# Six of eight tiles ahead in linear attention's out-projection, and root chains given other engines and delays

## The chip, the core and the metric

One core of one Trainium2 chip runs the kernel. Its engines are TensorE (PE, matrix products, with its weight loads shown apart as PEld), VectorE (DVE), ScalarE (ACT), GpSimd (POOL) and SyncE (SP, which here issues the loads of weights). The metric is the device time of one execution in microseconds (us), the median of several runs. Lower is better.

## The reference

A decoder trunk of two layers works on 512 tokens behind 16 meta tokens, 528 rows of width 1024, in float32. Layer 0 mixes tokens by gated linear attention in chunks (GLA, four heads), layer 1 by local attention with a window of 128, learned sinks and shared keys and values (SWA). Around each mixer stand two feed-forward blocks (FFN), and each sublayer is normalised at its input and at its output:

```
for layer in range(2):
    h = h + 0.5 * rmsnorm(swiglu(rmsnorm(h, g[0]), w_in0, w_out0), g[1])
    hn = rmsnorm(h, g[2])
    mix = gla_mixer(hn, ...) if layer == 0 else swa_mixer(hn, ...)
    h = h + rmsnorm(mix, g[3])
    h = h + 0.5 * rmsnorm(swiglu(rmsnorm(h, g[4]), w_in1, w_out1), g[5])
    if layer == 0:
        k_sh, v_sh = shared_kv(h, ...)

# the end of gla_mixer, per head of 256 columns
o = rmsnorm(o, g_head) * silu(r)
return o.reshape(B, L, 1024) @ w_out
```

`rmsnorm` divides by the root of the mean square over the columns. In `gla_mixer` that mean is taken for each head by itself.

## The kernel before

**Layout.** Columns lie on partitions, tokens along the free axis. A matrix of width 1024 is thus eight tiles of 128 partitions. In layer 0 the tokens are cut into two groups, `L0`, of 272 and 256; in layer 1 the norms use `L1`, two groups of 256, and the products mostly `L1W`, one of 512.

**Products.** Each float32 product is made of three matmuls of rounded halves (`mm3`): high weight by high input, low weight by high input, high weight by low input. The high half of an input or a weight is a copy by ACT (L413, L432, L228), the low half a subtraction by DVE (L414, L433, L229). The third matmul of a product needs the low half of the input.

**Order.** PE runs in the order in which the program emits its matmuls; nothing reorders them. The program is a planner: `Flow` keeps a clock that each emitted matmul moves forward by its own length, and side jobs, written as generators, yield a delay and are resumed when the clock has passed it. A job that yields 2.0 therefore emits its next matmul about 2 us of matrix work later, whether or not its input is there by then. If it isn't, PE stands still. The order on ACT, DVE, POOL and SP is made by a scheduler. PSUM gives eight banks in rotation, the weights have 32 slots and a ring of eight raw buffers filled by SP.

**A norm.** The squares of the tiles are made on ACT. With one part (`parts` of 1) all squares of a group end in one sum: ACT writes the first square into it (L405), the others go to a scratch tile (L408) and POOL adds them (L409). With two parts the last square stays alone in a second sum, so POOL has no last addition and PE sums two tiles. `rstd` then emits: the column sums by PE (`st_`), a chain of small steps for the reciprocal root (`av_`, `yv_`, `zv_`, `wv_`, L366 to L386), a diagonal matrix (`dg_`, L388), and, after a planned delay, a matmul that spreads the factors over the partitions (`r_`). The chain runs on POOL (then its first step is on ACT, L368; planned delay `CHAIN`, 5) or on DVE (`DCHAIN`, 3). `Operand.factors` uses it for the factor R of a block's input, copied from PSUM by ACT (L449), on POOL. `Residual.run` uses it on DVE for a block's output, and then for each of eight tiles multiplies and adds on DVE (L471, L472), makes the next input's halves (L432, L433) and its squares.

**The end of GLA.** The four heads' cores run one after the other while PE also projects `x` by the gate's weights, eight units of two groups (`x<-x_l0m`). For the last head (h = 3) the order is: the head's output in two banks (`po_`, copied to `Y` by ACT at L977) and a small one for the meta tokens (`pn`, copied by DVE at L980), squares, `st_go`, roots on POOL for both groups, `r_go` for both groups, and DVE's scaling of `Y` (L989). `gated` makes `rg` from the gate (L1005 to L1007), and when the head is scaled, multiplies by the gain and by `Y` (L1012) and splits the result into the halves of `og`, one for each of the eight tiles. The tiles 0 to 3 belong to heads 0 and 1 and wait for their cores; the tiles 4 to 7 all wait for the last head's. `flow.wait(*jobs)` ends this stage, and only then `out_proj` opens: each of its units takes eight tiles of `og` into one bank, 24 matmuls (`y<-og`).

**out_steps** can be told of jobs that are still open (`jobs`): it then opens the first three banks (m, group) with all tiles but the last, waits for these jobs, and goes on. GLA doesn't use this before the change.

**SWA.** `x_first` projects queries by unit; the first four need R (`r_l1m`) before DVE can make `q` from them (L1036 to L1039, with POOL). Scores (`sc`) go to PE between the rows of the next four units (`x<-x_l1m`), whose matmuls fill PE's time there. Then `out_proj` runs twice, and at its end the norm of its output `post_l1f`: group 0's tiles are finished first, then group 1's, so group 0's `Residual.run` goes on during group 1's products, and the next block's input `x_l1f` is made tile by tile.

Of the kernel before, what the change touches and what calls it, by code (L numbers as in the profile page):

```python
# [17 lines left out]
D = 1024  # L18
KD = 8
# [7 lines left out]
HEADS = 4  # L27
RSQRT_MAGIC = float(0x5F3759DF)
L0 = [(0, 272), (272, 256)]
L1 = [(16, 256), (272, 256)]  # L30
# [14 lines left out]
STAGGER = 5.0  # L45
SOFT = 5.0
ADDED = 1.4
BEHIND = 2.2
NORM = 3.0
LAG = 3  # L50
# [75 lines left out]
def trunk_kernel(ctx: ExitStack, tc, a, out):  # L126
    nc = tc.nc
    pe, act, dve, pool, sp = nc.tensor, nc.scalar, nc.vector, nc.gpsimd, nc.sync
    flow = Flow()
# [8 lines left out]
    Y = cp.tile([P, KD, TOK], F32, name="Y")  # L138
# [20 lines left out]
    def gain(layer, i, k):  # L159
        c = V_GAIN + layer * 48 + i * 8 + k  # L160
        return vec[:, c : c + 1]
# [43 lines left out]
    used, asked, freed, ahead, cap, dma_end = [0], [0], [0], [16], [len(units)], [0.0]  # L205
# [143 lines left out]
    def mm3(o, w, j, x, g, start, stop):  # L349
        mm3s([(o, w)], j, x, g, start, stop)  # L350
# [50 lines left out]
    def square_into(sums, src, i, count, name, parts=2):  # L401
        n = src.shape[-1]
        if i == 0 or i == count - 1 and parts == 2:
            sums.append(sm.tile([P, 272], F32, tag="acc", name=f"acc_{name}", bufs=6))
            act.activation(sums[-1][:, :n], src, AF.Square)  # L405
            return
        t = sm.tile([P, 272], F32, tag="sq", name=f"sq_{name}", bufs=2)
        act.activation(t[:, :n], src, AF.Square)  # L408
        pool.tensor_tensor(sums[0][:, :n], sums[0][:, :n], t[:, :n], op=ALU.add)  # L409
# [6 lines left out]
    class Operand:  # L416


        def __init__(self, name, gv, groups, rt=None, parts=(1, 2)):
            self.parts = parts  # L420
            self.name, self.gv, self.groups, self.tiles = name, gv, groups, [None] * KD
            self.ready = set()
            self.rt = rt
            self.rjob = [None] * len(groups)
            self.accs = [[] for _ in groups]
# [17 lines left out]
        def factors(self, gi, eng=pool):  # L443
            if self.rt is None:
                self.rt = sm.tile([P, TOK], F32, tag="R", name=f"R_{self.name}", bufs=2)
            o, n = self.groups[gi]
            yield FACT + (ADDED if self.parts[gi] == 1 else 0)
            r = yield from rstd(self.accs[gi], n, D, False, f"{self.name}_{o}", eng, gi * BEHIND if eng is dve else 0.0)
            act.activation(self.rt[:, o : o + n], r[:, :n], AF.Copy)  # L449

        def need(self, gi, k):
# [1 line left out]


    class Residual:
        def __init__(self, name, layer, i, half, nxt=None):
            self.name, self.half, self.nxt = name, half, nxt
            self.gain = lambda m: gain(layer, i, m)

        def run(self, gi, g, sums):  # L460
            o, n = g
            nxt = self.nxt
            yield 1.8 + (0 if gi else ADDED)
            r = yield from rstd(sums, n, D, self.half, f"post_{self.name}{gi}", dve)
            if nxt is None:
                yield from self.store(gi, g, r)
                return
            for k in range(KD):
                h, y = H[:, k, o : o + n], Y[:, k, o : o + n]
                t = r[:, 256 : 256 + n] if n <= 256 else ps(f"t_{self.name}{gi}{k}")[:, :n]  # L470
                dve.tensor_tensor(t, y, r[:, :n], op=ALU.mult)  # L471
                dve.tensor_tensor(h, t, h, op=ALU.add)  # L472
                nxt.build(gi, k)
                nxt.sumsq(gi, k)
                yield 1.0
            nxt.rjob[gi] = flow.spawn(nxt.factors(gi), gi * BEHIND)
# [81 lines left out]
    def out_proj(*args, **named):  # L558
        for _ in out_steps(*args, **named):
            pass  # L560

    def out_steps(hid, groups, split_groups, first, finish=None, tailm=0, packed=False, jobs=()):
        nh = len(hid)
        ws = []

        def tile_of(m, j):
            i, c = divmod(m * nh + j, 8) if packed else (m, j)
            while len(ws) <= i:
                ws.append(next_w())
            return ws[i], c  # L570

        begun = {}

        def begin(m, g):
            o, n = g
            p = begun[m, o] = ps(f"y{used[0]}_{m}_{o}")
            for j, t in enumerate(hid[:-1]):
                w, c = tile_of(m, j)
                mm3(p[:, :n], w, c, t, g, j == 0, False)

        def unit(m, g):
            o, n = g
            if (m, o) not in begun:
                begin(m, g)
            p = begun[m, o]
            w, c = tile_of(m, nh - 1)
            mm3(p[:, :n], w, c, hid[-1], g, nh == 1, True)
            y = Y[:, m, o : o + n]
            if first:
                act.activation(y, p[:, :n], AF.Copy)  # L590
            else:
                dve.tensor_tensor(y, p[:, :n], y, op=ALU.add)  # L592

        accs = [[], []] if finish else []

        def sq(m, gi):
            o, n = split_groups[gi]
            y = Y[:, m, o : o + n]
            square_into(accs[gi], y, m, KD, f"post{used[0]}_{m}_{gi}", gi + 1)
            act.activation(y, y, AF.Identity, scale=finish.gain(m))  # L600

        def through(m):
            return (m + 1) * nh // 8 if packed else m + 1

        freed = 0
        if jobs:
            order = [(m, g) for m in range(KD - tailm) for g in groups]
            order += [(m, split_groups[0]) for m in range(KD - tailm, KD)]
            begin(*order[0])
            yield  # L610
            for m, g in order[1 : 2 if order[1][1][1] == SEQ else 3]:
                begin(m, g)
            flow.wait(*jobs)
        for m in range(KD - tailm):
            for g in groups:
                unit(m, g)
            done_w(through(m) - freed)
            freed = through(m)
            for gi in range(len(accs)):
                sq(m, gi)  # L620
        if not finish:
            return
        for gi, g in enumerate(split_groups):
            for m in range(KD - tailm, KD):
                unit(m, g)
                sq(m, gi)
                if gi:
                    done_w(through(m) - freed)
                    freed = through(m)
            flow.spawn(finish.run(gi, g, accs[gi]))  # L630
# [187 lines left out]
    def gla(x, finish):  # L818
        set_ahead(10)
        with tc.tile_pool(name="gp", bufs=1) as gp:  # L820
# [59 lines left out]
            blk = lambda t: t[:, META:].rearrange("p (b c) -> p b c", c=P)  # L880

            def core(h, before):
                for j in before:
                    yield j
                tau = 1.0 / 16.0
# [7 lines left out]
                for i in range(2):  # L893
                    p = ps(f"pv{h}_{i}")
# [32 lines left out]
                p = ps(f"pk{h}")  # L927
# [13 lines left out]
                p = ps(f"pa{h}")  # L941
# [40 lines left out]
                for gi, (o, n) in enumerate(L0):  # L982
                    accs.append([])
                    for i in range(2):
                        square_into(accs[gi], Y[:, 2 * h + i, o : o + n], i, 2, f"go{h}_{gi}", 1)
                yield 2.0 + ADDED
                def scale(gi, o, n):
                    r = yield from rstd(accs[gi], n, 256, True, f"go{h}_{gi}", more=BEHIND)
                    dve.tensor_tensor(  # L989
                        yy[:, :, o : o + n], yy[:, :, o : o + n],  # L990
                        r[:, :n].unsqueeze(1).to_broadcast([P, 2, n]), op=ALU.mult,
                    )
# [32 lines left out]
            jobs = []  # L1025
            set_ahead(8)
            x_units(x, KD, L0, lambda i, g, p: jobs.append(flow.spawn(gated(i, g, p))))
            flow.wait(*jobs)
            set_ahead(16)
            cap[0] = used[0] + 12  # L1030
            out_proj(og, L0, L0, True, finish, 5)

    def rope(dst, p, c, s, name):
        n = dst.shape[-1]
# [244 lines left out]
    dve.memset(eps, 1e-6)  # L1279
    dve.tensor_scalar(hident, ident, 0.5, None, op0=ALU.mult)  # L1280

    def into(name, layer, i, half, gv, groups, parts=(1, 2)):
        nxt = Operand(name, gv, groups, parts=parts)
        return nxt, Residual(name, layer, i, half, nxt)


    nxt, fin = into("l0m", 0, 1, True, lambda k: gain(0, 2, k), L0, (1, 1))
# [9 lines left out]
    with tc.tile_pool(name="kp", bufs=1) as kp:  # L1297
        x = Operand("l1f0", lambda k: gain(1, 0, k), L1)

        def again(gi):  # L1300
            for k in range(KD):
                x.build(gi, k)
                yield 1.0

        kv, placed = shared_kv(nxt, kp, [again(0), again(1)])
        x.rt, x.rjob = nxt.rt, nxt.rjob
        nxt, fin = into("l1m", 1, 1, True, lambda k: gain(1, 2, k), L1, (1, 1))
        ffn(x, L1W, fin)
        x = nxt
        nxt, fin = into("l1f1", 1, 3, False, lambda k: gain(1, 4, k), L1)  # L1310
        flow.wait(placed)
        swa(x, kv, fin)
    ffn(nxt, L1W, Residual("out", 1, 5, True))
# [85 lines left out]
```

## Time and profile before

| what | value |
|---|---|
| time, median of 3 runs | 1918.19 us (1917.45 to 1920.05) |
| the profiled execution's own time | 1915.33 us |
| its span, first to last instruction | 1913.5 us |
| PE busy | 1872.4 us, 98% |
| DVE, ACT, POOL busy | 1420.2, 1002.8, 236.6 us |
| mean granted TensorE clock | 0.996 |

The profiled execution is 2.86 us below the median, and 1.83 us of its time lie around the span. In a timeline row stand the start, the length, the engine, the line, the operation, the written tile and the read ones, the shape, how many such instructions follow each other, and in brackets how long the engine had been idle and what ended it. In a row of waits stand the total, the number of times and the longest. In a row by windows stand the window, its length, the busy time of each engine with its count, the granted clock, the share of DMA and its rate.

### The profile page before, as it was taken

To read this page: it belongs to the slowest core of one execution; us is meant where nothing else is said; L and a number is where in the kernel's file an instruction comes from. 1 tells how busy PE (TensorE), PEld (TensorE's weight loads), DVE (VectorE), ACT (ScalarE), POOL (GpSimd) and SP (SyncE) were. 2 spreads that over 40 slices of the span, in tenths; PEclk is the share of its full clock that TensorE was granted. 3 is DMA by queue.
4 is the path that set the end of the run, shared out by engine and by line. 5 is a ranking of instruction groups with operands and counts; after the bars stand their busy time and mean duration, and the time that the engine had idled before them with its cause. 6 is when DMAs were issued, how large, how long until landed. Compare 5 with 4: busy or idle time off the path is not lost.

```text
span 1913.5 us, 37141 instructions
## 1 busy us (share of the span) xinstructions
PE 1872.4 (98%) x14374; PEld 1786.8 (93%) x14374; DVE 1420.2 (74%) x2868; ACT 1002.8 (52%) x2268; POOL 236.6 (12%) x439
## 2 busy tenths in 40 slices
PE   8999999999999999999999999999998999999997
PEld 8999999999998999999999898989976888989897
DVE  7885858775564798585887886868789578868584
ACT  5663636663245566363674553536646555536363
POOL 2000000321122400000034000000361140000002
PEclk9999999999999999999999999999999999999999
DMA  4332333322123123233351223233320212233331
GB/s 165 99 101 94 101 99 102 120 78 78 45 59 108 45 79 101 93 102 97 102 170 45 67 91 113 91 108 110 118 78 23 78 45 72 95 105 106 105 116 45
DMA packets 102017, 174.60 MB, mean 91 GB/s; under 512 B 11345, under 2 KB 24145, under 8 KB 101841
## 3 DMA queue, kind: packets, MB, share of 16 engines
q1 hardware_dynamic: 101008, 171.59, 28.4%
q8 instruction: 112, 1.84, 0.4%
q10 hardware_dynamic: 832, 0.65, 0.1%
q14 instruction: 65, 0.52, 0.1%
HBM read 170.10 MB, written 2.10 MB: 90 GB/s over the span
## 4 chain that ended last, share of the span: by engine, by line
PE 79%; DVE 13%; ACT 3%; issue 2%; POOL 1%; DMA 0%; DVEq 0%; ACTq 0%; POOLq 0%
PE y L164 29%; PE a L164 18%; PE x L164 14%; PE c L164 8%; PE d L164 4%; DVE raw L253 2%; DVE w L229 2%; ACT w_s L247 1%; DVE w_s L248 1%; DVE w L248 1%; PE e L164 1%; PE o L164 1%; PE po L164 1%; PE ps L164 0%; DVE H L472 0%
## 5 line engine op out<-in xcount | busy, mean ns | idle before, releaser
L248 DVE TENSOR_TENSOR w_s<-raw,w_s 128x512 fp32r<-128x512 f32 x288 | 193.9, 690 | 124.4 <-ACT w_s L247 122.4
L164 PE MATMUL y<-hidl0f,w 128*128 128x256 f32 (+1 forms) x2112 | 261.7, 285 | 0.8 <-DVE hidl0f L414 0.6
L164 PEld LDWEIGHTS y<-hidl0f,w 128*128 128x128 f32 x2112 | 258.9, 188 | 1.6 <-DVE hidl0f L414 1.0
L229 DVE TENSOR_TENSOR w<-raw,w 128x512 fp32r<-128x512 f32 x378 | 242.1, 670 | 17.7 <-ACT w L228 15.8
L247 ACT ACTIVATE w_s<-raw 128x512 fp32r<-128x512 f32 x288 | 175.3, 628 | 146.0 <-DVE raw L253 142.4
L164 PE MATMUL y<-hidl1f,w 128*128 128x512 f32 (+1 forms) x1344 | 249.9, 346 | 0.3
L164 PEld LDWEIGHTS y<-hidl1f,w 128*128 128x128 f32 x1344 | 212.7, 188 | 33.6 <-DVE hidl1f L811 0.7
L409 POOL TENSOR_TENSOR acc_post<-acc_post,sq_post 128x256 f32<-128x256 f32 (+1 forms) x78 | 63.3, 811 | 1360.2 <-ACT sq_post L408 1359.7
L228 ACT ACTIVATE w<-raw 128x512 fp32r<-128x512 f32 x378 | 208.0, 586 | 36.9 <-PE y L164 26.0
L253 DVE TENSOR_TENSOR raw<-raw,raw 128x512 f32<-128x512 f32 x288 | 197.9, 687 | 5.5
L248 DVE TENSOR_TENSOR w<-raw,w 128x512 fp32r<-128x512 f32 x216 | 148.3, 687 | 40.0 <-ACT w L247 39.1
L247 ACT ACTIVATE w<-raw 128x512 fp32r<-128x512 f32 x216 | 134.0, 621 | 48.0 <-PE y L164 47.7
L164 PE MATMUL x<-x_l0m,w 128*128 128x272 f32 (+1 forms) x1200 | 158.1, 288 | 0.0
L164 PEld LDWEIGHTS x<-x_l0m,w 128*128 128x128 f32 x1200 | 149.2, 188 | 1.0
L592 DVE TENSOR_TENSOR Y<-y,Y 128x256 f32<-128x256 f32 (+2 forms) x176 | 82.3, 473 | 76.6 <-PE y L164 75.9
L164 PE MATMUL a<-zl0f_t,w_s 128*128 128x264 f32 x864 | 117.5, 285 | 0.0
L164 PE MATMUL a<-zl1f_t,w_s 128*128 128x256 f32 x864 | 114.7, 282 | 0.9 <-ACT c L786 0.7
L164 PEld LDWEIGHTS a<-zl0f_t,w_s 128*128 128x128 f32 x864 | 110.3, 188 | 0.3
L164 PEld LDWEIGHTS a<-zl1f_t,w_s 128*128 128x128 f32 x864 | 107.5, 188 | 2.3 <-ACT c L786 1.7
L164 PE MATMUL x<-x_l0f,w 128*128 128x256 f32 (+1 forms) x768 | 99.5, 290 | 7.6 <-ACT w L228 6.4
L164 PEld LDWEIGHTS x<-x_l0f,w 128*128 128x128 f32 x768 | 96.4, 191 | 8.8 <-ACT w L228 6.4
L164 PE MATMUL x<-x_l1f,w 128*128 128x256 f32 (+1 forms) x576 | 94.0, 321 | 1.9 <-ACT x_l1f L432 1.8
(485 smaller groups left out, 3290.7 us busy)
## 6 DMA issues: line engine op xcount, KB each, us to landing
raw<-in_w_in SPq DMA_DIRECT2D x352, 256.0 KB, 2.9
raw<-in_w_out SPq DMA_DIRECT2D x96, 256.0 KB, 3.4
raw<-in_gla_in SPq DMA_DIRECT2D x50, 256.0 KB, 3.4
raw<-in_w_last SPq DMA_DIRECT2D x48, 256.0 KB, 3.0
raw<-in_w_out SPq DMA_DIRECT2D x64, 128.0 KB, 3.0
raw<-in_gla_out SPq DMA_DIRECT2D x16, 256.0 KB, 2.7
raw<-in_w_q SPq DMA_DIRECT2D x16, 256.0 KB, 4.0
raw<-in_swa_out SPq DMA_DIRECT2D x16, 256.0 KB, 2.8
```

What stands on the lines that cost most here:

```text
L164: inst = pe.matmul(o, lhs, rhs, start=start, stop=stop, skip_group_check=onto)
L228: act.activation(w[:, 0, :m], raw[:, :m], AF.Copy)
L229: dve.tensor_tensor(w[:, 1, :m], raw[:, :m], w[:, 0, :m].bitcast(F32), op=ALU.subtract)
L247: act.activation(w[:, 0, :512], src, AF.Copy)
L248: dve.tensor_tensor(w[:, 1, :512], src, w[:, 0, :512].bitcast(F32), op=ALU.subtract)
L253: dve.tensor_tensor(dst, dst, src, op=ALU.add)
L409: pool.tensor_tensor(sums[0][:, :n], sums[0][:, :n], t[:, :n], op=ALU.add)
L592: dve.tensor_tensor(y, p[:, :n], y, op=ALU.add)
```

## The change

It has four parts.

- `LONGER`, 0.8, is added to the planned delay of a root chain on POOL in `Operand.factors`. The `r_` matmul of every block input that has its chain there is emitted later by that much matrix work.
- `Residual` gets its own `parts`, and `into` a parameter for them (`post`). For the norm of the local attention's output it is (2, 2) in place of (1, 2): group 0's squares end in two sums, and its `st_` is planned 1.4 us sooner. The other norms keep (1, 2).
- For the last head of GLA the squares end in two sums for both groups, `st_go` is planned 1.4 us sooner, and the roots run on DVE, both groups' steps taking turns, with the delay of DVE's chains and 2.2 more for the second group.
- GLA waits only for the first twelve jobs (tiles 0 to 5) before `out_proj`, which gets the open jobs and `late=2`: the first three banks are opened with six tiles each, the last two tiles of each follow.

```
+LONGER = 0.8
 class Operand / factors:
-            r = yield from rstd(..., eng, gi * BEHIND if eng is dve else 0.0)
+            r = yield from rstd(..., eng, gi * BEHIND if eng is dve else LONGER)
 class Residual:
-        def __init__(self, name, layer, i, half, nxt=None):
+        def __init__(self, name, layer, i, half, nxt=None, parts=(1, 2)):
+            self.parts = parts
-            yield 1.8 + (0 if gi else ADDED)
+            yield 1.8 + (ADDED if self.parts[gi] == 1 else 0)
 out_steps:
-    def out_steps(hid, groups, split_groups, first, finish=None, tailm=0, packed=False, jobs=()):
+    def out_steps(hid, groups, split_groups, first, finish=None, tailm=0, packed=False, jobs=(), late=1):
-            for j, t in enumerate(hid[:-1]):
+            for j, t in enumerate(hid[:-late]):
-            w, c = tile_of(m, nh - 1)
-            mm3(p[:, :n], w, c, hid[-1], g, nh == 1, True)
+            for j in range(nh - late, nh):
+                w, c = tile_of(m, j)
+                mm3(p[:, :n], w, c, hid[j], g, j == 0, j == nh - 1)
-            square_into(accs[gi], y, m, KD, f"post{used[0]}_{m}_{gi}", gi + 1)
+            square_into(accs[gi], y, m, KD, f"post{used[0]}_{m}_{gi}", finish.parts[gi])
 gla / core:
+                last = h == HEADS - 1
-                        square_into(accs[gi], Y[:, 2 * h + i, o : o + n], i, 2, f"go{h}_{gi}", 1)
-                yield 2.0 + ADDED
+                        square_into(accs[gi], Y[:, 2 * h + i, o : o + n], i, 2, f"go{h}_{gi}", 1 + last)
+                yield 2.0 + (0 if last else ADDED)
-                    r = yield from rstd(accs[gi], n, 256, True, f"go{h}_{gi}", more=BEHIND)
+                    eng, more = (dve, gi * BEHIND) if last else (pool, BEHIND)
+                    r = yield from rstd(accs[gi], n, 256, True, f"go{h}_{gi}", eng, more)
 gla, its end:
-            flow.wait(*jobs)
+            flow.wait(*jobs[:12])
-            out_proj(og, L0, L0, True, finish, 5)
+            out_proj(og, L0, L0, True, finish, 5, jobs=jobs, late=2)
 the calls:
-    def into(name, layer, i, half, gv, groups, parts=(1, 2)):
+    def into(name, layer, i, half, gv, groups, parts=(1, 2), post=(1, 2)):
-        return nxt, Residual(name, layer, i, half, nxt)
+        return nxt, Residual(name, layer, i, half, nxt, post)
-        nxt, fin = into("l1f1", 1, 3, False, lambda k: gain(1, 4, k), L1)
+        nxt, fin = into("l1f1", 1, 3, False, lambda k: gain(1, 4, k), L1, post=(2, 2))
```

More of the change, by code (lines that the diff above doesn't have):

```diff
@@ L447, in factors @@
             yield FACT + (ADDED if self.parts[gi] == 1 else 0)
-            r = yield from rstd(self.accs[gi], n, D, False, f"{self.name}_{o}", eng, gi * BEHIND if eng is dve else 0.0)
+            r = yield from rstd(self.accs[gi], n, D, False, f"{self.name}_{o}", eng, gi * BEHIND if eng is dve else LONGER)
             act.activation(self.rt[:, o : o + n], r[:, :n], AF.Copy)
```

## The prediction

> **What bounds the kernel now.** I read the page's busy shares, then PE's waits, then the timeline at the three places that the change touches, and the granted clock there by windows. First the page and the waits of PE:
>
> ```profile
> PE 1872.4 (98%) x14374; PEld 1786.8 (93%) x14374; DVE 1420.2 (74%) x2868; ACT 1002.8 (52%) x2268; POOL 236.6 (12%) x439
> ...
> PE 79%; DVE 13%; ACT 3%; issue 2%; POOL 1%; DMA 0%; DVEq 0%; ACTq 0%; POOLq 0%
> ```
>
> ```profile
> PE r_go L164 <- POOL dg_go L388: 4.2, 1, 4.2
> ...
> PE x L164 <- ACT x_l1f L432: 1.8, 2, 1.3
> PE sc L164 <- DVE q L1037: 1.6, 1, 1.6
> ...
> PE r_post_l1f L164 <- DVE dg_post_l1f L388: 0.8, 1, 0.8
> ...
> PE r_kv L164 <- POOL dg_kv L388: 0.5, 1, 0.5
> PE r_l0f L164 <- POOL dg_l0f L388: 0.3, 1, 0.3
> ```
>
> PE is busy 98% of the span, and 79% of the chain that ended last is PE. The matrix work stays but for a few small column sums. So what can be won is idle PE, a few microseconds out of 1913.5, and it is worth its full length where PE is what ends the stage. The longest wait that the change can touch is the last GLA head's `r_go`, 4.2 us. The clock, by windows (window, length, then busy us of PE, PEld, DVE, ACT, POOL, granted clock, DMA share, rate):
>
> ```profile
> 577.80:581.20 3.40, 0.73 (x2) 0.30 (x2) 0.75 (x3) 1.03 (x4) 3.22 (x12) 1.00 0.49 154
> 581.20:584.60 3.40, 3.36 (x13) 3.18 (x14) 2.78 (x7) 0.00 (x0) 0.00 (x0) 0.50 0.00 0
> ...
> 1420.90:1424.30 3.40, 1.76 (x11) 1.05 (x10) 3.40 (x9) 1.46 (x5) 3.24 (x5) 1.00 0.51 154
> 1424.30:1427.70 3.40, 3.40 (x11) 2.33 (x11) 3.40 (x6) 1.16 (x4) 3.32 (x3) 0.50 0.22 77
> ```
>
> Behind the idle stretch at `r_go` PE ran 3.4 us at half clock, and again in the attention behind a stretch in which it was busy 1.76 of 3.40 us. Each such window costs half of its 3.4 us, 1.7 us of work.
>
> [...]
>
> **A. The end of GLA.** The timeline of PE, then of the other engines:
>
> ```profile
> 568.04 0.39 PE L164 MATMUL pn<-am,vm 16*128 16x16 f32 x2
> 568.36 5.01 PE L164 MATMUL x<-x_l0m,w 128*128 128x272 f32 x39
> 573.21 1.04 PE L164 MATMUL st_go<-ones,acc_go 128*68 128x1 f32 x12
> 574.11 2.06 PE L164 MATMUL x<-x_l0m,w 128*128 128x256 f32 x15
> 580.40 2.06 PE L164 MATMUL r_go<-dg_go,ones 68*128 68x272 f32 x4 [4.23 <-POOL dg_go L388]
> 581.90 4.11 PE L164 MATMUL y<-og,w 128*128 128x272 f32 x20
> ...
> 586.19 10.02 PE L164 MATMUL y<-og,w 128*128 128x272 f32 x78 [0.17 <-DVE og L414]
> ```
>
> ```profile
> 569.04 0.78 DVE L1005 TENSOR_TENSOR rg<-x,R_l0m 128x272 f32<-128x272 f32 x2 [0.38 <-PE x L164]
> ...
> 574.18 0.19 POOL L369 TENSOR_SCALAR yv_go<-av_go 68x4 int32<-68x4 int32 x1 [3.13 <-ACT av_go L368]
> ...
> 579.71 0.64 POOL L388 TENSOR_TENSOR dg_go<-hident,yv_go 68x272 f32<-68x272 f32 x1
> ...
> 581.16 0.72 DVE L989 TENSOR_TENSOR Y<-Y,r_go 128x544 f32<-128x544 f32 x1 [2.65 <-PE r_go L164]
> ...
> 583.11 1.12 DVE L414 TENSOR_TENSOR og<-rg,og 128x272 fp32r<-128x272 f32 x3
> ```
>
> What is lost there now: the `x` row of 39 takes 573.21 - 568.36 = 4.85 us, 0.124 us a matmul. From the end of `x` (574.11 + 2.06 = 576.17) to the end of the `y` row (586.19 + 10.02 = 596.21) are 20.04 us. In them lie four records of `r_go`, about 0.5 us at that rate, and 98 matmuls of `y` (20 and 78), 12.2 us. So 7.3 us are lost: 4.2 in the wait for POOL, 1.7 by the half clock, the rest inside `r_go` and on `og`.
>
> POOL's chain is why: 574.18 to 580.35 is 6.2 us for two groups, with 2.1 us of `x` as its cover. After the change the chain is on DVE. Of DVE's chain for one group the trace shows the first and last of ten steps and the diagonal, and one pair of independent small steps:
>
> ```profile
> 381.32 0.16 DVE L366 TENSOR_SCALAR av_post_l0m<-st_post_l0m 128x2 f32<-128x2 f32 x1 [1.68 <-PE st_post_l0m L164]
> ...
> 383.29 0.43 DVE L388 TENSOR_TENSOR dg_post_l0m<-hident,yv_post_l0m 128x256 f32<-128x256 f32 x1
> ```
>
> ```profile
> 431.27 0.16 DVE L913 TENSOR_TENSOR f<-b 128x16 f32<-128x16 f32 x1
> 431.36 0.54 DVE L914 TENSOR_TENSOR f<-b 128x384 f32<-128x384 f32 x1
> ```
>
> A group takes 383.29 - 381.32 = 1.97 us and 0.43. Two groups whose steps take turns take between 1.97 us (each second step fits into the gap of the first, as the 0.09 us between L913 and L914 suggests) and 3.94 us (each step waits for the one in front). With 0.2 us of hand-over that is 2.6 to 4.6 us from `st_go` to `dg_go`. In the built order 27 matmuls of `x` stand between `pn` and `st_go` and 21 between `st_go` and `r_go`: 21 x 0.124 = 2.6 us of cover. The wait at `r_go` is then 0 to 2.0 us; I take 0.3, since the nearer row is the pair of independent steps.
>
> Then PE meets `og`. In DVE's built order the low half of tile 4 stands behind `rg` of unit 7 (two of L1005, 0.78), both scalings of `Y` (0.72 and about 0.7) and two gate steps between them (0.4 each), and takes 0.42 itself (a third of the 1.12 row, rounded up): 3.5 us after the last `x`. PE gets there after two `r_go` (0.5) and 14 matmuls (1.7): 1.3 us of waiting, and 0.4 on tile 5, two subtractions later. The tiles 6 and 7 are needed only after 54 matmuls (6.7 us), and by the same steps are there about 2 us sooner. This is what the six-tile opening is worth: it covers the last head's own tiles, not the halves of tiles 4 and 5, which are queued behind its scaling. `st_go` doubles from 12 records to 24, at (574.11 - 573.21) / 12 = 0.075 us: +0.9. POOL's 26 lost instructions and the ACT steps gone are worth nothing by themselves, as nobody else waits for them there. The raw buffers of the pair of weights that ACT now splits ahead of the last `po_` copy were issued some 25 us earlier, and SP's order stays but for one small load; I cost both at 0, and up to 0.5 if ACT is held up.
>
> Sum of A: -7.3 + 0.9 + 0.3 + 1.3 + 0.4 = -4.4 us. Best end, without waits beyond 0.5: -5.9. Worst, with a wait of 2.0, 1.8 on `og` and 0.5 on ACT: -2.1.
>
> [...]
>
> **B. `LONGER`.** `r_l0f` and `r_kv` stand 0.8 us later and no longer wait for POOL: -0.3 and -0.5 by the rows of waits above. The others had no wait at their `r_`, and R comes that much later to DVE, with eight banks behind it. -0.8, which is the best end too; the worst is 0.
>
> **C. The attention's opening.** The same delay puts `r_l1m` of the second group six matmuls later.
>
> ```profile
> 1407.10 5.78 PE L164 MATMUL x<-x_l1m,w 128*128 128x512 f32 x24
> ...
> 1410.69 0.61 POOL L388 TENSOR_TENSOR dg_l1m<-ident,yv_l1m 128x256 f32<-128x256 f32 x1
> 1410.85 0.01 DVE L1036 LOAD_MASK_SELECT sh_q<-x  x1 [3.51 <-PE x L164]
> ...
> 1419.57 2.25 DVE L229 TENSOR_TENSOR w<-raw,w 128x512 fp32r<-128x512 f32 x2
> ...
> 1424.03 2.35 PE L164 MATMUL sc<-kz,q 64*128 64x272 f32 x8 [1.64 <-DVE q L1037]
> ```
>
> Here `dg_l1m` was ready at 1411.30 and there was nothing to win: six matmuls at 5.78 / 24 = 0.24 us are 1.4 us by which R and DVE's work behind it come later. Against that, one pair of weights (2.25 us of DVE) now stands ahead of R, in the 3.51 us in which DVE was idle. So the late `q` for which PE waited 1.64 us comes 2.25 - 1.4 = 0.8 us sooner: -0.8. Best end: the wait and the half-clock window behind it both go, -3.3. Worst: the lateness stays, +1.4.
>
> **D. The norm behind the attention.**
>
> ```profile
> 1565.24 1.61 PEld L164 LDWEIGHTS x<-x_l1f,w 128*128 128x128 f32 x12 [0.69 <-ACT x_l1f L432]
> ...
> 1567.18 1.47 PEld L164 LDWEIGHTS x<-x_l1f,w 128*128 128x128 f32 x12 [0.34 <-ACT x_l1f L432]
> ```
>
> ```profile
> 1564.37 0.42 ACT L408 ACTIVATE sq_l1f<-H 128x256 f32<-128x256 f32 x1 [2.52 <-POOL acc_l1f L409]
> ...
> 1570.14 3.09 PE L164 MATMUL x<-x_l1f,w 128*128 128x256 f32 x18 [1.28 <-ACT x_l1f L432]
> ```
>
> ACT stood 2.52 us behind POOL, which was running group 0's root chain for `l1f`, and PE then waited three times for tiles of group 1, 0.69 + 0.34 + 1.28 = 2.3 us. With two sums POOL has one addition less, and group 0's `st_` and `r_post_` stand 15 matmuls earlier, 1.8 us at 0.12. Group 0's tiles and the root chain then end some 2 us sooner and ACT is free: the three waits go. Two more column sums are four records, 0.3 us at the 0.075 above; I take 0.4, as all are of the larger shape. The 0.8 us at the second `r_post_l1f` stays, its chain is not moved. -2.3 + 0.4 = -1.9; ends -2.3, and +0.5 if ACT is late again and only the records are added.
>
> **Sum.** -4.4 - 0.8 - 0.8 - 1.9 = -7.9 us against the profiled execution's own 1915.33, so 1907.4. That execution lies 2.86 us below the median of the runs; -7.9 from 1918.19 gives 1910.3, which I predict.
>
> **Rivals.** (1) DVE's two chains cost twice one, so `r_go` still waits 2.0 us, and the halves of tile 4 come as late: A is -2.8, the sum -6.3, 1911.9. For it: the pair L913/L914 had no dependence on a step just before. (2) The attention gives it back. DVE is without a gap there from R on; R is 1.4 late, the two rows of `x` that stand earlier (3 matmuls each, 1.4 us) are missing as fillers later, and one more half-clock window (1.7) is drawn: C is +4.5, the sum -2.6, 1915.6, within 0.2%. Against it: the 2.25 us moved out of the way. (3) Slower: in the attention the stalls of PE grow by the missing fillers so that windows of 3.4 us fall to half use and more, as at 1420.90. Each costs 1.7 us. With R late and the fillers gone (2.8) and five such windows (8.5), C is +11.3 and the sum +4.2: 1922.4. With three windows the gain is gone (+0.8), with five it is slower by over 0.2%. Against it: the trace shows one such window in the attention although several stalls of over a microsecond stand there.
>
> [...]
>
> **How the numbers follow.** The forecast has 0.58, (1) 0.16, (2) 0.15, (3) 0.11. 0.2% of 1918.19 is 3.8 us, about what a measurement can tell from no change; faster means below 1914.4. Forecast and (1) are faster: 0.74 with little left over; (2) is the same, 0.15; (3) slower, 0.11. The ends of A to D add up to -12.3 (1905.9) and -0.2 (1918.0), where all would have to fall the same way; the range 1906.0 to 1917.0 leaves out those corners and (3). The likeliest case alone has 1907.5 to 1913.
>
> **What would show it.** A: `r_go` with a wait under 0.5 us, none by POOL; the granted clock at 1.00 behind it; 1.7 us of waits of `y` on `og` in two or three pieces, on tiles 4 and 5. B: `r_l0f` and `r_kv` gone from PE's waits. C: DVE's weight pair in front of R; `sc` waiting under 1 us. D: no `x` waiting on `x_l1f`, and ACT no longer 2.5 us behind POOL. It goes wrong if the halves of `og` come later than 3.5 us after `x`, if the stalls of the attention grow behind the later R, or if a new half-clock window appears.

## The result and the profile after

The changed kernel takes 1910.58 us (median of 5 runs, 1909.31 to 1911.01) against 1917.52 us (median of 5 runs, 1916.36 to 1920.05): 6.9 us less, a ratio of 0.9961 with a 95% interval from 0.9946 to 0.9975. The forecast was 1910.3 us, by a sum of -7.9 us. The profiled execution took 1910.46 us, its span is 1908.6 us.

From its page, the busy shares and the chain that ended last, by engine:

```profile
PE 1873.1 (98%) x14390; PEld 1789.5 (94%) x14390; DVE 1423.5 (75%) x2890; ACT 1001.4 (52%) x2266; POOL 228.2 (12%) x412
...
PE 86%; DVE 10%; ACT 2%; issue 1%; DMA 0%; SPq 0%; DVEq 0%; ACTq 0%
```

PE runs 16 matmuls more, the column sums, and is busy 0.7 us more in a span 4.9 us shorter. Its share of the chain grew from 79% to 86%, and POOL's 1% is gone. PE's waits, only those of the places in question, first of the changed kernel, then two of the kernel before:

```profile
PE ptm L177 <- DVE mt L1176: 4.8, 1, 4.8
...
PE sc L165 <- DVE Y L1158: 2.0, 1, 2.0
PE r_post_l1f L165 <- DVE dg_post_l1f L389: 1.4, 1, 1.4
...
PE y L165 <- DVE hidl0f L415: 0.9, 3, 0.3
```

```profile
PE ptm L176 <- DVE mt L1171: 3.8, 2, 2.4
...
PE y L164 <- DVE hidl0f L414: 0.6, 2, 0.3
```

The waits of `r_go`, `r_kv` and `r_l0f` and the two of `x` on `x_l1f` are no longer in the list. New or longer are, in the attention, one of 4.8 us for `mt` in place of two, one of `sc` for DVE's `Y`, 2.0 us, in place of the 1.6 for `q`, and those of `x` for ACT's tiles of `x_l1m`, 1.2 us in place of 0.7; further the second `r_post_l1f`, 1.4 us in place of 0.8, and `y` for the FFN's hidden tiles, 0.9 in place of 0.6. The end of GLA on PE:

```profile
569.05 3.55 PE L165 MATMUL x<-x_l0m,w 128*128 128x272 f32 x27
572.44 1.98 PE L165 MATMUL st_go<-ones,acc_go 128*68 128x1 f32 x24
574.28 2.79 PE L165 MATMUL x<-x_l0m,w 128*128 128x256 f32 x21
576.94 1.16 PE L165 MATMUL r_go<-dg_go,ones 68*128 68x272 f32 x4
577.75 2.12 PE L165 MATMUL y<-og,w 128*128 128x272 f32 x14
580.23 13.95 PE L165 MATMUL y<-og,w 128*128 128x272 f32 x110 [0.36 <-DVE og L415]
```

And on the other engines, DVE's chain (the first row is the second group's first step, each row of two is one step of both groups) and what follows it:

```profile
574.53 0.16 DVE L367 TENSOR_SCALAR av_go<-st_go 128x2 f32<-128x2 f32 x1 [0.81 <-PE st_go L165]
574.61 0.36 DVE L370 TENSOR_SCALAR yv_go<-av_go 68x4 int32<-68x4 int32 x2
...
576.46 0.77 DVE L389 TENSOR_TENSOR dg_go<-hident,yv_go 68x272 f32<-68x272 f32 x2
577.14 0.76 DVE L1010 TENSOR_TENSOR rg<-x,R_l0m 128x272 f32<-128x272 f32 x2
577.83 0.71 DVE L994 TENSOR_TENSOR Y<-Y,r_go 128x544 f32<-128x544 f32 x1
...
579.14 0.68 DVE L994 TENSOR_TENSOR Y<-Y,r_go 128x512 f32<-128x512 f32 x1
579.74 1.45 DVE L415 TENSOR_TENSOR og<-rg,og 128x272 fp32r<-128x272 f32 x4
```

From the second group's first step to the first diagonal are 576.46 - 574.53 = 1.93 us, in which the steps of both groups run, as long as one group took alone (1.97). `r_go` has no wait, and `y` one of 0.36 us, where 14 matmuls in it meets the low half of tile 4, which stands behind `rg` and the two scalings.

To see where the time went, I took the start of the same matmul in two timelines and subtracted. The table gives that against the first profile of the kernel before, in us, negative for sooner; the differences between lines are what a stage won or lost. The matmuls of a name are counted from 0:

| matmul | changed kernel | its repeat | kernel before, repeat |
|---|---|---|---|
| `x` in the middle of GLA (x_l0m, 600th, at 469 us) | -0.19 | -0.26 | +0.81 |
| `y<-og`, 96th (behind the opening) | -5.26 | -5.34 | +0.90 |
| last `x<-x_l0f` | -5.90 | -5.98 | +0.92 |
| first `x<-x_kv` | -5.03 | -5.11 | +0.88 |
| first `y<-hidl1f` | -5.88 | -5.95 | +0.84 |
| `x<-x_l1m`, 144th (before the attention) | -5.96 | -6.04 | +0.84 |
| `y<-so`, 36th (behind the scores) | -3.46 | -4.84 | +2.48 |
| `y<-so`, 143rd | -3.51 | -4.89 | +2.49 |
| last `x<-x_l1f` (behind the norm) | -5.10 | -6.47 | +2.46 |
| last `y<-hidl1f` | -5.40 | -6.77 | +2.51 |

Four stages stand out: GLA -5.1, the two delays -0.7 net, the attention +2.5 in one execution and +1.2 in the other, the norm -1.6. Behind the last product the changed kernel loses 0.5 us again, and its repeat 0.4. The table holds one execution each; the repeats are the first two experiments.

### The profile page after: what moved, and what is told of

The parts are those of the page before. It is cut to its first block, busy times and chain, and to the rows that moved or that the text cites. A ratio compares the mean times of both kernels' runs of the same rounds, so it can differ in the third digit from the quotient of the medians.

```text
span 1908.6 us, 37171 instructions
## 1 busy us (share of the span) xinstructions
PE 1873.1 (98%) x14390; PEld 1789.5 (94%) x14390; DVE 1423.5 (75%) x2890; ACT 1001.4 (52%) x2266; POOL 228.2 (12%) x412
## 4 chain that ended last, share of the span: by engine, by line
PE 86%; DVE 10%; ACT 2%; issue 1%; DMA 0%; SPq 0%; DVEq 0%; ACTq 0%
PE y L165 30%; PE a L165 19%; PE x L165 17%; PE c L165 8%; PE d L165 5%; DVE raw L254 1%; DVE w L230 1%; PE o L165 1%; ACT w_s L248 1%; DVE w_s L249 1%; PE e L165 1%; DVE w L249 1%; PE po L165 1%; PE ps L165 0%; PE sc L165 0%
```

## The experiments

Theory: each of the four stages won or lost by its own part of the change. Rivals: what is won early is lost later; and the attention's loss is not the order but the phase of the clock's windows.

**The changed kernel again, and the kernel before again.** No edit.

> The changed kernel once more. In the two traces the stages moved PE by -5.0 us at the end of GLA, -0.6 by the two longer delays, +2.5 between the opening of the attention and its end, and -1.6 at the norm behind it. Theory 1 (the later R gives it back): the attention's +2.5 us comes again to within 0.5 us, as it lies in the order. Theory 2 (the phase of the clock's windows): the changed kernel had three halved windows there and the kernel before one; in a new execution the grid of 3.4 us windows falls elsewhere, and the attention's loss changes by 1.7 us for each halved window more or less, while the other three stages stay within 0.3 us.

> The kernel before once more. Its first profiled execution had one halved window in the attention and was 2.8 us below the median of its 17 runs (1915.33 to 1918.14). If the attention's loss is the phase of the windows, another execution has two or three halved windows there, its attention ends 1.5 to 3 us later than in the first, all else within 0.3 us, and its time is 1916.5 to 1919. If the first execution was typical, the attention ends within 0.5 us of it.

The changed kernel: 1909.53 us (5 runs, 1909.05 to 1911.05) against 1918.14 (17 runs, 1915.34 to 1920.13), ratio 0.9955, 0.9942 to 0.9967. The kernel before: 1918.30 us in one run. In the first profiles of the two kernels the stretches at half clock begin whole multiples of 3.413 us apart (843.09 us in the kernel before, at 581.21 and 1424.30 us; 34.13 and 17.07 us in the changed kernel, at 1398.20, 1432.33 and 1449.40 us: 247, 10 and 5 windows); windows cut at such times are called the grid from here on. By windows of it, first the changed kernel's first profile, then its repeat (PE's busy time is the first figure behind the length, the granted clock stands behind POOL's):

```profile
1394.80:1398.20 3.40, 1.55 (x11) 1.14 (x10) 3.40 (x5) 2.38 (x6) 3.24 (x4) 1.00 0.48 166
1398.20:1401.60 3.40, 2.94 (x9) 2.56 (x10) 3.40 (x7) 1.03 (x2) 0.12 (x1) 0.50 0.72 215
...
1446.00:1449.40 3.40, 0.23 (x2) 0.27 (x3) 3.40 (x8) 0.52 (x3) 2.87 (x3) 1.00 0.00 0
1449.40:1452.80 3.40, 3.40 (x27) 3.07 (x26) 3.40 (x8) 0.28 (x1) 0.52 (x1) 0.50 0.00 0
```

```profile
1393.44:1396.85 3.41, 2.17 (x18) 1.96 (x17) 3.41 (x6) 2.30 (x6) 3.33 (x4) 1.00 0.33 96
1396.85:1400.27 3.42, 2.34 (x15) 1.96 (x14) 3.42 (x6) 2.31 (x5) 1.32 (x2) 1.00 0.67 217
```

The same two waits ahead of the attention fell into one window of the grid in the first execution, which was busy 1.55 of 3.4 us, and the next was halved; in the repeat they fell across two, and none was. That is the 1.4 us between the two columns: 1.3 of it arise at the matmuls of `x` under the halved window. The kernel before, repeat, at GLA's end and in the attention:

```profile
576.36:579.77 3.41, 0.61 (x6) 0.41 (x4) 2.66 (x6) 2.51 (x7) 3.17 (x12) 1.00 0.18 50
579.77:583.18 3.41, 1.97 (x5) 1.45 (x6) 0.66 (x1) 0.00 (x0) 2.06 (x8) 0.50 0.31 104
583.18:586.60 3.42, 3.42 (x17) 3.42 (x16) 3.29 (x10) 0.72 (x2) 0.00 (x0) 0.50 0.00 0
...
1450.17:1453.58 3.41, 1.06 (x7) 0.35 (x5) 3.41 (x15) 2.64 (x16) 0.33 (x1) 1.00 0.01 2
1453.58:1457.00 3.42, 3.42 (x24) 3.09 (x26) 3.00 (x8) 0.28 (x1) 2.21 (x3) 0.50 0.00 0
```

Here two windows were halved behind `r_go` in place of one, which cost only 0.1 us (+0.81 to +0.90 in the table), and a second one in the attention, which ended 1.6 us later than in the first profile. So the first profile of before was a lucky one, and 1.6 us of the attention's +2.5 was the comparison with it. Of the rest of the 3.0 us between the two spans, 0.8 came at the kernel's opening, where PE waits for the first weights, and 0.5 behind the last product, so "all else within 0.3 us" did not hold.

**The longer delay in layer 0 alone.**

```
-            ... gi * BEHIND if eng is dve else LONGER)
+            ... gi * BEHIND if eng is dve else LONGER * (self.groups is L0))
```

> The longer delay of root chains on GpSimd only in layer 0, none in layer 1; all else as in the changed kernel. Theory 1 (the later R of the attention gives back 2.5 us): the attention runs as in the kernel before, the waits at the first reciprocal factors of layer 1 do not come back as there were none, and the time is about 2 to 2.5 us below the changed kernel's, some 9 us below before. Theory 2 (phase of the windows): no difference from the changed kernel beyond 1.7 us either way, about 7 us below before.

1912.52 us (7 runs, 1911.71 to 1914.08), ratio 0.9974, 0.9963 to 0.9984: 3.0 us slower than the repeat on the same chip. So the later R is no loss by these runs. What it is worth in the attention they don't show: this execution had 10.2 us at half clock there (three windows, the repeat two) and lost 2.5 us, 1.3 more than the repeat; 1.2 more were lost behind the last product. The norm won 0.9 us in place of 1.6. ACT's timeline there, of this kernel and of the changed one:

```profile
1559.49 0.36 ACT L450 ACTIVATE R_l1f<-r_l1f 128x256 f32<-128x256 f32 x1
...
1560.39 1.28 ACT L649 ACT_TABLE_LOAD   x1
...
1562.53 0.49 ACT L433 ACTIVATE x_l1f<-H,vec 128x256 fp32r<-128x256 f32 x1
```

```profile
1562.45 0.36 ACT L450 ACTIVATE R_l1f<-r_l1f 128x256 f32<-128x256 f32 x1
1562.72 0.50 ACT L433 ACTIVATE x_l1f<-H,vec 128x256 fp32r<-128x256 f32 x1
...
1563.76 1.28 ACT L649 ACT_TABLE_LOAD   x1
```

With the delay R comes later, and the work that R releases on ACT, a table load of 1.28 us ahead of the first gate, stands behind the last tile of `x_l1f`. Without it, it stands ahead of the last two (one is shown), and PE waits 1.1 us for one.

**The end of GLA alone, and all but it.** The first has `LONGER = 0.0` and no `post`; the second has the lines of GLA as before.

> Only the end of GLA is changed (two sums, roots on VectorE, the six-tile opening); no longer delay, and one sum for the local attention's norm. Theory of separate stages: -5.0 us against before, all at the end of GLA; the waits for GpSimd at r_l0f and r_kv (0.3 and 0.5 us), the attention with its wait of sc for q, and the three waits for tiles of x_l1f are as before. Rival (the gain is lost later): less than -3.5 us, because a later stage waits longer by what it was reached earlier.

> All of the change but the end of GLA, which is as before. Theory of separate stages: -0.6 (two waits for GpSimd) +2.5 (attention) -1.6 (norm) = about +0.3 us against before; the wait of 4.2 us at r_go and the halved window behind it are back. Rival (the attention's loss was the phase of the windows): -0.5 to -3 us.

GLA alone: 1911.65 us (5 runs, 1909.69 to 1912.79), ratio 0.9965, 0.9952 to 0.9977. By the same subtraction its GLA stage wins 5.2 us, the norm 0.0, and the waits of `x` on `x_l1f` are 1.8 us in two as before. All but GLA: 1915.21 us (11 runs, 1914.70 to 1916.38), ratio 0.9985, 0.9976 to 0.9994; the norm wins 1.6 us there too. So the gain of GLA is kept. The stages are separate but for one coupling that the theory left out: in all but GLA the GLA stage itself ended 0.8 us later than in the kernel before. GLA's own R has the longer delay too, the heads' work came 0.8 us later against `x`, 9 matmuls of `x` were left behind `st_go` in place of 15, and `r_go` waited 4.7 us in place of 4.2. In the changed kernel this costs 0.15 us (5.2 won without the delay, 5.1 with it). The second was expected at +0.3 by the theory and came to -2.9 by the medians, on the rival's side: again the first profile of before as the base.

**Roots without the opening, opening without the roots.**

```
-            flow.wait(*jobs[:12])
+            flow.wait(*jobs)
-            out_proj(og, L0, L0, True, finish, 5, jobs=jobs, late=2)
+            out_proj(og, L0, L0, True, finish, 5)
```

```
-                        square_into(..., f"go{h}_{gi}", 1 + last)
+                        square_into(..., f"go{h}_{gi}", 1)
-                yield 2.0 + (0 if last else ADDED)
+                yield 2.0 + ADDED
-                    eng, more = (dve, gi * BEHIND) if last else (pool, BEHIND)
+                    eng, more = (pool, BEHIND)
```

> As the changed kernel, but the out-projection of GLA opens only after the last tile, each bank with all eight tiles at once; roots on VectorE and two sums stay. Theory (roots and opening share the gain): r_go still waits under 0.5 us, but PE meets tile 6 after 18 matmuls (2.2 us) in place of 54 (6.7 us), while its halves come some 5 us after r_go: a wait of about 2.5 us on the tiles 6 and 7, and the GLA stage gains -2.5 us in place of -5.0. Rival (the roots alone do it): -4.5 to -5.0. Rival (the opening alone does it): 0 to -1.

> As the changed kernel, but the last head's roots on GpSimd with one sum, as before; the six-tile opening stays. Theory: tiles 4 and 5 too are finished in the plan only behind r_go, so nothing of the opening can stand ahead of the wait of 4.2 us and of the halved window; only the later waits on the tiles go: -0.5 to -1.5 us at the GLA stage. Rival (the opening alone does it): -3 us or more.

Without the opening: 1912.48 us (7 runs, 1910.70 to 1912.77), ratio 0.9972, 0.9961 to 0.9983; the GLA stage wins 3.2 us. With roots on POOL: 1914.48 us (11 runs, 1913.74 to 1915.68), ratio 0.9984, 0.9975 to 0.9993, like all but GLA. PE's timeline of the two:

```profile
577.01 1.16 PE L165 MATMUL r_go<-dg_go,ones 68*128 68x272 f32 x4
577.82 2.11 PE L165 MATMUL y<-og,w 128*128 128x272 f32 x14
580.29 1.08 PE L165 MATMUL y<-og,w 128*128 128x272 f32 x4 [0.36 <-DVE og L415]
582.18 0.51 PE L165 MATMUL y<-og,w 128*128 128x272 f32 x2 [0.82 <-ACT og L414]
```

```profile
581.20 2.13 PE L165 MATMUL r_go<-dg_go,ones 68*128 68x272 f32 x4 [4.72 <-POOL dg_go L389]
582.76 9.50 PE L165 MATMUL y<-og,w 128*128 128x272 f32 x57
```

The first meets tile 6 after 18 matmuls and waits for its high half; the opening is worth 5.1 - 3.2 = 1.9 us. The second wins nothing at GLA, whose stage ends 0.8 us late just as in all but GLA: the opening stands behind `r_go`, and there is no long wait on a tile left for it to cover. It was expected to win 0.5 to 1.5.

**One sum for the local attention's norm.** `post=(2, 2)` taken out.

> As the changed kernel, but one sum for the first group of the local attention's norm, as before. Theory (the sooner first group gives the 1.6 us there): the three waits of x for tiles of x_l1f are back in part, at least 1 us of the 1.6 is lost at that norm, and the rest of the kernel is as changed; the delay of the next block's factors still removes up to 0.7 us. Rival (the delay alone gives it): the norm stage stays at -1.6 us.

1911.23 us (5 runs, 1910.83 to 1912.51), ratio 0.9968, 0.9956 to 0.9981. The norm still wins 1.2 us of the 1.6: 0.4 is lost, not 1 or more. With the 0.9 of the two sums without the delay, either does more than half of the work alone.

**Tiles 4 and 5 finished sooner; the second `r_post_l1f` later.**

```
-                yield cores[m // 2 if m < 4 else 3]
+                yield cores[m // 2 if m < 6 else 3]
```

```
-            r = yield from rstd(sums, n, D, self.half, f"post_{self.name}{gi}", dve)
+            r = yield from rstd(sums, n, D, self.half, f"post_{self.name}{gi}", dve, 1.4 * (self.parts == (2, 2) and gi))
```

> As the changed kernel, but the tiles 4 and 5 of og are finished behind head 2's core, to which their columns belong, and not behind the last head's. In the changed kernel y waits 0.5 us on the low half of tile 4 (some 0.7 us in all), as it is queued on VectorE behind the last head's scaling. Theory (that queue is the wait): the wait goes, the GLA stage gains 0.4 to 0.7 us more, and the rest is as changed. Rival: VectorE's work moved ahead of the last head's states and roots delays po or r_go by as much or more, 0 to +0.7 us.

> As the changed kernel, but the second group's r_ matmul of the local attention's norm is planned 1.4 us later (12 matmuls of 128x256). In the changed kernel PE waits 1.6 us there for VectorE's diagonal. Theory (PE can use the time for products that are ready): the wait falls under 0.3 us and the norm stage gains about 1.2 us more. Rival (the products moved ahead are missing behind it): the tiles of the second group come no sooner, PE waits for them by as much, and the stage gains under 0.3 us.

1910.41 us (5 runs, 1910.08 to 1910.71; ratio 0.9959, 0.9946 to 0.9971) and 1911.09 us (5 runs, 1910.89 to 1912.70; ratio 0.9964, 0.9950 to 0.9977): neither beats the changed kernel. In the first the wait on tile 4 is gone, but DVE's work for it now stands ahead of head 3's core, PE waits 1.3 us for DVE's `f` there, and GLA wins 4.6 us, 0.5 less: the rival. In the second the wait at `r_post_l1f` is gone and the norm wins 2.3 us, 0.7 more; of the 1.4 us the tiles took back 0.5 by one wait:

```profile
1563.26 5.90 PE L165 MATMUL x<-x_l1f,w 128*128 128x256 f32 x36 [0.46 <-ACT x_l1f L433]
```

The last FFN then lost 1.3 us by new waits, two of them of 0.4 us, whose cause was not followed.

**PE kept busy during a wait.** In the changed kernel at the third `ptm`, where PE waits 4.8 us, and in the kernel before at `r_go`. Both add products of constants into a bank that is overwritten at once:

```
+                for _ in range(19 if u == 2 else 0):
+                    pe.matmul(pm[:, :P], ones, ident, start=True, stop=True)
                 transpose(pm[:, :P], mt.rearrange("p c m -> p (c m)"))
```

```
         r = ps(f"r_{name}")
+        for _ in range(17 if name == "go3_0" else 0):
+            pe.matmul(r[:, :P], ones, ident, start=True, stop=True)
```

> As the changed kernel, with 19 extra products of constants (128x128, float32, some 0.22 us each, 4.2 us in all) on TensorE in front of the third ptm of the attention, where it waits 4.9 us for VectorE anyway; they write a bank that is overwritten at once. Theory (a window in which TensorE is half idle or more halves the next): the halved window behind that wait goes, the one behind the earlier wait of 2.1 us stays, and the attention ends up to 1.7 us sooner; less if VectorE sets its end. Rival (the halving has another cause): the same number of halved windows.

> The kernel before, with 17 such products (3.7 us) on TensorE in front of the last GLA head's r_go, where it waits 4.4 us for GpSimd. Theory: the halved window or two behind that wait go, and the GLA stage gains 1.7 to 2.7 us although the wait itself is as long as before; so this much of the 5.0 us that the change wins there is the clock. Rival: the halved windows stay or cost nothing, 0 to -0.3 us.

At `r_go`: 1917.88 us (11 runs, 1914.91 to 1918.47) against 1918.87, ratio 0.9994, 0.9985 to 1.0003, not to be told from no change. By its profile no window was halved there, and the stage won 1.3 us against the first profile of before (one halved window) and 1.4 against the repeat (two), although `r_go` came no sooner; 1.7 to 2.7 had been expected:

```profile
575.92 3.96 PE L397 MATMUL r_go<-ident,ones 128*128 128x128 f32 x34
580.98 1.54 PE L164 MATMUL r_go<-dg_go,ones 68*128 68x272 f32 x4 [1.09 <-POOL dg_go L388]
```

At `ptm`: 1912.34 us (6 runs, 1912.07 to 1912.55), ratio 0.9970, 0.9958 to 0.9981, above the changed kernel's 0.9961 and 0.9955, though the intervals overlap. The halved window behind the wait is gone, and yet nothing is won: the attention lost 3.8 us against the first profile of before, the repeat with as many halved windows 1.2. By windows, then PE's next wait in this kernel and in the changed kernel's repeat:

```profile
1444.64:1448.06 3.42, 3.14 (x29) 2.96 (x28) 3.42 (x9) 0.72 (x5) 2.89 (x3) 1.00 0.00 0
1448.06:1451.47 3.41, 3.41 (x50) 3.07 (x50) 3.41 (x9) 0.48 (x2) 0.73 (x1) 1.00 0.02 5
1454.87:1458.28 3.41, 0.88 (x12) 0.64 (x12) 3.00 (x8) 2.10 (x9) 1.04 (x1) 1.00 0.00 0
1458.28:1461.69 3.41, 3.19 (x27) 3.20 (x28) 0.97 (x5) 0.00 (x0) 0.00 (x0) 0.50 0.47 154
```

```profile
1456.56 0.45 PE L165 MATMUL o<-pt,vt 128*64 128x128 f32 x4 [2.95 <-DVE pt L1199]
```

```profile
1456.49 0.45 PE L165 MATMUL o<-pt,vt 128*64 128x128 f32 x4 [1.43 <-DVE pt L1197]
```

PE got there 1.5 us sooner, waited 1.5 us longer, and went on at the same time, since DVE's `pt` set it. A later window was then halved, and PE waited 1.1 us for DVE's next `pt`, which had two weight halves ahead of it; together they put it 2.6 us behind the repeat. DVE's order there is another one than in the changed kernel, so this run doesn't price a halved window alone.

## Why the prediction was right, point by point

**A, the end of GLA: -4.4 forecast, -5.1 measured.** The mechanism and its parts held. `r_go` waits for nothing: the two chains took 1.93 us, the lower of the two bounds. In the trace the steps of the two chains start 0.08 to 0.13 us apart, but for one pair, and take 0.15 to 0.17 us each, so that a step of one chain starts before the step of the other has ended. The mis-sized term is the wait on `og`, forecast 1.7 us, and 0.7 by gaps between starts (0.36 us in the row): tile 4's low half came 580.1 - 576.9 = 3.2 us behind the last `x`, not 3.5, and PE got there 0.3 us later than I had it. The doubled column sums cost 574.28 - 572.44 = 1.84 in place of 0.90, as forecast. The clock's part, put at 1.7 us, is 1.3 to 1.4 by the run with PE kept busy. The coupling with GLA's own R, 0.15 us, was put at nothing. Which part does what: roots and two sums 3.2, the opening 1.9 more, the opening alone nothing.

**B, the delay: -0.8 forecast, -0.7 measured, of which 0.25 came with GLA alone too.** It won 0.6 and 0.9 at the two `r_`, more than their waits, but the first is back by the first `x<-x_kv`: 0.9 us are lost there, 0.7 of them at one `y`, since behind the later R the FFN's hidden tiles came later. "R comes that much later, with eight banks behind it" was the step that failed.

**C, the attention: -0.8 forecast, +2.5 in the first profile and +1.2 in its repeat; what the order alone is worth stays open.** Against the first profile of before, which had one halved window in this stage, executions with the old order lost 0.3, 1.6 and 2.1 us with two (the kernel before with PE kept busy at `r_go`, its repeat, GLA alone) and 2.5 with three (the delay in layer 0 alone). With the new order they lost 1.1, 1.2, 1.2 and 1.5 with two (the tiles sooner, one sum, the repeat, all but GLA), 1.4 and 2.5 with three, 2.8 and 2.9 with four. At the same number of windows the two orders overlap, so neither the sign nor the size of the forecast is shown. Of its steps, the weights in front of R (six halves in a row, before four) and the wait of `sc` for `q` went as forecast. But `sc` then waits 2.0 us for `Y`, not under 1, the tiles of `x_l1m` cost 0.5 us more, and the rows of `x` that stand earlier are used up 11 us sooner (the last one at 1437.9, before at 1449.3), so that one wait of 4.8 us for `mt` took the place of two. The second rival described this. The third rival's halved windows did come, two to four in an execution, not five.

**D, the norm: -1.9 forecast, -1.6 measured.** The waits went. The 2.3 us put on them came in part from rows of weight loads; PE's own two waits were 1.8 us, which would have made the sum -1.4. The forecast gave it all to the sooner first group. The delay, which I had costed at nothing here, does most of it alone (1.2 us), by keeping the table load behind the last tile; together they give 1.6. "The 0.8 us at the second `r_post_l1f` stays" was wrong, it grew to 1.4: DVE's scheduler put two weight halves between the steps of that chain. Without the delay in layer 1 they stand elsewhere, and the wait is 0.5 us. The long small step in the first row is no part of it; one of 0.71 us stood there before too:

```profile
1546.70 0.70 DVE L374 TENSOR_SCALAR wv_post_l1f<-zv_post_l1f 128x2 f32<-128x2 f32 x1
...
1548.72 0.69 DVE L230 TENSOR_TENSOR w<-raw,w 128x512 fp32r<-128x512 f32 x1
...
1549.40 0.68 DVE L230 TENSOR_TENSOR w<-raw,w 128x512 fp32r<-128x512 f32 x1
```

**The sum.** -7.9 forecast; -6.9 by the first medians and -8.6 by the repeat, each with an interval of about 2.5 us either way. A, B and D add up to -7.4 in both profiles of the changed kernel, and the experiments tell them apart. That the median came within 0.3 us of the forecast is in part luck: the forecast stood on a median of three runs that is 0.7 us above that of five, A won 0.7 more than forecast, and C did not show the 0.8 it was to win. That the profiled execution of before was 2.9 us below its median was said in the forecast, but not why; against the repeat, 1.6 us of it was the clock's phase in the attention, 0.8 the first weights and 0.5 the end behind the last product.

## What to carry to other kernels

Where an engine runs in an order fixed by a plan, look for the chain that a wait hangs on, move it to the engine that is free at that moment, and give what is already finished something to do behind it: here the two together won 5 us, the cover without the faster chain nothing. Before a loss or a gain of one or two microseconds in a stage is put down to the order, compare profiles with the same number of half-clock windows, or take the profile again. A later factor can be a gain, here of 1.2 us at the norm: what it releases on another engine is then queued behind the tiles that are needed first.

## What the runs showed of the hardware that I had not expected

The clock was at half (0.50 granted) for the whole next window of the grid behind windows in which PE was busy for 0.23 to 1.78 us of 3.41, none of them idle. The first profile of the changed kernel has four windows, between 20 and 1890 us, in which PE was busy for less than 1.9 us: behind those with 1.55, 1.45 and 0.23 us the next was halved, behind one with 1.83 us (1442.57 to 1445.99) it was not. That of the kernel before has four there too: the windows with 0.73 and 1.76 us that the prediction shows were followed by a halved one, and two with 1.77 and 1.88 us were not. In the repeat of the changed kernel a halved one followed 1.52 and 0.27 us, in that of the kernel before 0.61 (two halved), 1.78 and 1.06 us, with the longer delay in layer 0 alone 1.03 us (two halved, 1430.80 to 1437.60), with PE kept busy at `ptm` 0.88 us. What decides between 1.76 and 1.78 us on the one side and 1.77, 1.83 and 1.88 us on the other these traces don't show. The two windows of the kernel before that no halved one followed, each with the window behind it:

```profile
574.39:577.80 3.41, 1.77 (x15) 1.57 (x13) 1.95 (x5) 2.21 (x6) 2.85 (x12) 1.00 0.21 76
577.80:581.21 3.41, 0.73 (x2) 0.30 (x2) 0.76 (x3) 1.03 (x4) 3.22 (x12) 1.00 0.49 154
1400.41:1403.82 3.41, 1.88 (x14) 1.47 (x12) 3.41 (x5) 2.38 (x5) 3.25 (x4) 1.00 0.56 175
1403.82:1407.24 3.42, 3.16 (x18) 2.78 (x19) 3.42 (x7) 0.00 (x0) 0.79 (x1) 1.00 0.58 181
```

The windows lie elsewhere in the kernel from one execution to the next: in two executions of the changed kernel, halved ones begin at 1398.20 and at 1430.99 us, 9.6 windows apart.

So the changed kernel had three or two halved windows in the attention and the kernel before one or two, and that moved an execution by 1.4 and 1.6 us. A halved window cost 1.3 and 1.4 us where PE set the pace (at `r_go`, ahead of the attention), and 0.1 us where the next wait was for DVE (the second one behind `r_go`).
